# Loading, gating and splitting the first two token tiles ahead of their output products, and four staging halves for W_out

## The chip, the cores and the metric

The kernel runs on one core of a Trainium2 chip. The metric is the device time of one execution in microseconds (us). TensorE is called PE in the profile, VectorE DVE, ScalarE ACT, GpSimd POOL, SyncE SP; SP issues all the large transfers in this program and its queue is shown as SPq. The kernel before took 683.60, 685.08 and 685.92 us in three runs, median 685.08.

## The reference

One step of a one-layer hybrid encoder. Each token row of x is projected once into the queries, keys and values of three groups of heads and into a gate of 1024 columns; the three attentions give 256 + 512 + 256 mixed columns, and these times the gate go through W_out into a residual and a LayerNorm. Cut to what matters here:

```
mixed = concat([o_a (256), o_b (512), o_m (256)], -1)      # o_b: RMS-normed per head, times subln_g
y     = einsum('bse,ed->bsd', mixed * silu(gate), w_out)   # 1024 x 1024
out   = layer_norm(DEEPNORM_ALPHA * x + y, ln_g, ln_b)
```

There are 1024 prompt tokens and 128 sample tokens, so nine tiles of 128 tokens, t = 0 to 8 (tile 8 holds the sample). Everything is float32.

## The kernel before

Every product of float32 matrices is done as three PE products of halves: an operand is split into a "hi" part (a cast, done by ACT) and a "lo" part (operand minus hi, done by DVE or POOL), and hi*hi, lo*hi and hi*lo are added in PSUM. Attention runs over eight units of two heads in the order M0, B0 to B3, A0, A1, M1. While PE works on one unit, the projections of what comes next are merged into it as a filler (`merge`). The instructions are emitted in that order and a list scheduler then fixes the order on each engine; on the chip each engine takes its instructions strictly in that order and waits on semaphores.

The last unit, M1 (`attention_m`, slot 7 of the mixed columns), works in four pairs of token tiles. Per pair: scores on PE, a maximum on DVE (L747), exp on ACT (L749), transposes on PE (L457), a split of these (`pth`, `ptl`, L460 and L461), products with the values into the one PSUM room `po` (L659), and `close_pair`, in which ACT copies half of `po` (L641) and DVE adds the halves (L644), which makes `po` free for the next pair. M1's filler is: two gate blocks in three chunks of 384 tokens (L142 to L144), each ended by tanh and a multiplication and a store to DRAM (`gates<-t`, L432); after each chunk c a call `load_wout(c)`; then the output products of tiles 0 and 1 (`out_steps`). Tiles 2 to 8 follow in a plain loop.

An output tile needs, in this order: the gates (`gscr`) and the mixed columns of seven slots (`oscr`) loaded from DRAM (L982, L984), the RMS factors (L986); the four slots of group B scaled by these (L987, DVE); mixed times gate for slots 0 to 6 (L995, DVE for t < 2, POOL after); slot 7 from M1's output, which is still in SBUF (L998); then `whi` (cast, ACT, L992) and `wlo` (subtraction, DVE, L993). The PE products are L1028, 2 x 8 x 3 per tile, each 128x512; then the residual sum and the statistics (L1035, L1036) and `norm`.

```
 gt = sp.tile(..., tag="kc") if t == 0 else pp.tile(..., tag="p")     # L981
 mx = op_.tile(..., tag="tab0") if t == 0 else pp.tile(..., tag="p")  # L983
```

For t = 1 both live in the pool `p`, whose six rooms hold the attention's probabilities. `mixed(t)` with its loads is called by the first of a tile's eight filler steps (`start(t)`).

`load_wout(c)` (L1074 to L1083) loads three rows of 128 of W_out (two for c = 2) in halves of 128x512 into a staging room `wraw` with two buffers, casts each half on ACT (L1082) and subtracts on DVE (first half) or POOL (second half, L1083). The splits end in x's room, tag `x{h,l}{c}`, free once the gates of chunk c have used x.

Of the kernel before, what the change touches and what calls it, by code (L numbers as in the profile page):

```python
# [7 lines left out]
F32 = mybir.dt.float32  # L8
F32R = mybir.dt.float32r
AF = mybir.ActivationFunctionType  # L10
ALU = mybir.AluOpType
# [4 lines left out]
P = 128  # L16
KT = 8
NTOK = 1152
NPR = 1024
CH = 384  # L20
# [24 lines left out]
SP = mybir.EngineType.SP  # L45
GATES = [2, 3, 4, 5, 0, 1, 6, 7]
SWAP = [i ^ 1 for i in range(32)]


class Pool:  # L50
# [4 lines left out]
    def __init__(self, pool):  # L55
        self.pool = pool
# [6 lines left out]
def hybrid_step(tc, d, o):  # L63
    nc = tc.nc
# [5 lines left out]
    def f(ap):  # L70
        return ap.bitcast(F32)

    const = pool("const")
    wst = pool("wst", 2)
# [7 lines left out]
    oscr = dram.tile([9, P, 7, P], F32, tag="mixed")  # L82
    gscr = dram.tile([9, P, 8, P], F32, tag="gates")
    mkscr = dram.tile([P, 256], F32, tag="mk")
    mvscr = dram.tile([P, 256], F32, tag="mv")
    rscr = dram.tile([9, 4, P], F32, tag="rstd")
# [19 lines left out]
    op_ = pool("opnd")  # L106
# [77 lines left out]
        nc.vector.tensor_tensor(out=u.va[:, :, :, 64:128], in0=v, in1=f(u.va[:, :, :, 0:64]), op=ALU.subtract)  # L184

    xp = pool("xp", 1, side="right")
    xh, xl = zip(*[[xp.tile([P, KT, CH], F32R, tag=f"x{i}{c}") for i in "hl"] for c in range(3)])


    cos = op_.tile([P, NTOK], F32, tag="tab0")  # L190
# [784 lines left out]
        return out  # L975


    def mixed(t):

        ts_ = slice(t * P, (t + 1) * P)  # L980
        gt = sp.tile([P, KT, P], F32, tag="kc") if t == 0 else pp.tile([P, KT, P], F32, tag="p")  # L981
        nc.sync.dma_start(gt, gscr[t])  # L982
        mx = op_.tile([P, 7, P], F32, tag="tab0") if t == 0 else pp.tile([P, 7, P], F32, tag="p")  # L983
        nc.sync.dma_start(mx, oscr[t])  # L984
        rs = tmp.tile([P, 4, P], F32, tag="rs", bufs=2)
        nc.sync.dma_start(rs, rscr[t].rearrange("(o k) c -> o k c", o=1).broadcast_to([P, 4, P]))  # L986
        nc.vector.scalar_tensor_tensor(  # L987
            out=mx[:, 2:6], in0=mx[:, 2:6], scalar=subg, in1=rs, op0=ALU.mult, op1=ALU.mult)
        mh, ml = [wst.tile([P, KT, P], F32R, tag=tag) for tag in ("whi", "wlo")]

        def parts(k):
            nc.scalar.copy(mh[:, k], gt[:, k])  # L992
            nc.vector.tensor_tensor(out=ml[:, k], in0=gt[:, k], in1=f(mh[:, k]), op=ALU.subtract)  # L993

        (nc.vector if t < 2 else nc.gpsimd).tensor_tensor(out=gt[:, 0:7], in0=mx, in1=gt[:, 0:7], op=ALU.mult)  # L995

        def last():
            nc.vector.tensor_tensor(out=gt[:, 7], in0=units[7].out[:, ts_], in1=gt[:, 7], op=ALU.mult)  # L998
            parts(slice(7, 8) if t < 2 else slice(0, 8))

        if t < 2:
            parts(slice(0, 7))
        else:
            last()
        return mh, ml, last

    outs = {}

    def start(t):
        u = outs[t] = Unit()  # L1010
        u.m = mixed(t)
        u.st = small.tile([P, 3, 6], F32, tag="st", bufs=2)

    def residual(t):
        u = outs[t]
# [54 lines left out]


    woh, wol = {}, {}

    def load_wout(c):  # L1074
        room = [xp.tile([P, 3, 1024], F32R, tag=f"x{i}{c}") for i in "hl"]
        for k in range(3 * c, min(3 * c + 3, KT)):
            hi, lo = woh[k], wol[k] = [r[:, k - 3 * c] for r in room]
            for n in range(2):
                s = slice(512 * n, 512 * n + 512)
                raw = wst.tile([P, 512], F32, tag="wraw")  # L1080
                nc.sync.dma_start(raw, d["wout"][k, :, s])
                nc.scalar.copy(hi[:, s], raw)  # L1082
                (nc.gpsimd if n else nc.vector).tensor_tensor(out=lo[:, s], in0=raw, in1=f(hi[:, s]), op=ALU.subtract)  # L1083

    def out_steps(t, u):

        st = {}

        def go(k):
            if k == 0:  # L1090
                start(t)
                if t == 0:
                    scales()
                st["y"] = [ps_p.tile([P, 512], F32, tag="pp") for _ in CUTS]
            if k == KT - 1:
                outs[t].m[2]()
            for cut, y in zip(CUTS, st["y"]):
                products(t, cut, y, k)
            if k == KT - 1:
                residual(t)  # L1100
                for n, (cut, y) in enumerate(zip(CUTS, st["y"])):
                    add(t, n, cut, y)
                norm(t)

        steps = [(1.4, lambda k=k: go(k)) for k in range(KT - 1)]
        return steps + [(1.4, lambda: go(KT - 1), lambda: t // 2 in u.closed)]
# [8 lines left out]
    stages = []  # L1115
    late = []
    first = [q_of(units[0])] + [gate_block(next(gates)) for _ in range(NG[0])]
    for parts in zip(*first):
        for part in parts:
            emit(part)  # L1120
    for i, u in enumerate(units):
        nxt = units[i + 1] if i + 1 < len(units) else None
        emit(with_stages(sum(k_of(u), []), EV))
        if u.kind != "M":
            while stages:
                stage()
            flush_tiny()
        if u.kind == "B":
            vb, ve = v_block(u, 14 + u.idx, o["bvT"][u.idx], 0)
        elif u.kind == "A":  # L1130
            tables_a(u)
            vb, ve = v_block(u, 4 + u.idx, o["avT"][u.idx], 512)
        else:
            vb, ve = [], []
        more = []
        gs = [gate_block(next(gates)) for _ in range(NG[i] if i else 0)]
        if nxt:
            more += sum(sum(gs, []), [])
        if nxt:
            more += sum(q_of(nxt), [])  # L1140
            fill = vb + more[:4] + ve + more[4:]
            if i == 6:
                stages = sample_of(u)
                fill = fill[:ES] + with_stages(fill[ES:], EV)
            if u.kind == "M":
                fill = with_stages(fill, 8)
        else:

            fill = []
            for c in range(3):  # L1150
                for g in gs:
                    fill += g[c]
                fill.append((0.0, lambda c=c: load_wout(c)))
            fill += out_steps(0, u) + out_steps(1, u)

        def need(kt, u=u, fill=fill):
            while u.vdone <= kt // 3:
                fill.pop(0)[1]()

        main = {"M": lambda: attention_m(u), "B": lambda: attention_b(u, need), "A": lambda: attention_a(u, need)}[u.kind]()  # L1160
        merge(main, fill, LEAD if u.kind != "M" else 1.0, RR if nxt else RL)
        if i != 6:
            ended = late[:]
            late.clear()
            now = sample_of(u)
            stages = stages + now[:LW] + ended + now[LW:]
        else:
            while stages:
                stage()
            flush_tiny()  # L1170
    for t in range(2, 9):
        start(t)
        residual(t)
        for n, cut in enumerate(CUTS if t < 8 else TAIL):
            if stages:
                stage()
            piece(t, n, cut)
        norm(t)
# [84 lines left out]
```

## Time and profile before

| what | value |
|---|---|
| three runs | 683.60, 685.08, 685.92 us (median 685.08) |
| profiled execution | 685.8 us, span 684.0 us |
| PE busy in the span | 662.8 us (97%) |
| DVE, ACT, POOL busy | 472.6, 356.3, 233.5 us (69%, 52%, 34%) |
| PE products L1028, all tiles | 37.5 + 37.0 + 37.1 us in 288 matmuls |
| idle of PE ahead of L1028 | 4.5 us (released by ACT, `whi` L992) and 1.4 us (released by DVE) |

How to read it: each engine's busy time is a share of one span, so a share of 97% says that PE is the engine to look at, and not where its 3% are. The slices of the page, then the table of stretches, then the single instructions say where. In a row of the timeline the brackets give how long the engine was idle ahead of that instruction and what released it.

### The profile page before, as it was taken

How to read it: one execution, taken by the hardware profiler on the slowest of the kernel's cores; microseconds unless marked ns; L12 is line 12 of the kernel's file. 1: busy time of each engine (PE TensorE's matmuls, PEld its weight loads, DVE VectorE, ACT ScalarE, POOL GpSimd, SP SyncE). 2: the span in 40 equal slices, each digit the busy share in tenths (PEclk: the TensorE clock that was granted, in tenths of full speed). 3: DMA queues.
4: the chain of work that ended last, by engine and by line, in shares of the span. 5: the costliest groups of instructions: out<-in, count | busy, mean ns of one | idle time of the engine just before them, and what ended most of it. 6: DMA issues, size and time to landing. Idle time of an engine off the chain costs nothing. (4 is left out here: it accounts for less than half of the span.)

```text
span 684.0 us, 12210 instructions
## 1 busy us (share of the span) xinstructions
PE 662.8 (97%) x4306; PEld 614.2 (90%) x4306; DVE 472.6 (69%) x1169; ACT 356.3 (52%) x922; POOL 233.5 (34%) x282
## 2 busy tenths in 40 slices
PE   8899999999999999999999999999999996999995
PEld 7789999999999999999999999999999985787884
DVE  4869966796579856897566435673666678677854
ACT  5748845566446645565456535764566684111000
POOL 7654212632344224532323433323133231324102
PEclk9999999999999999999999999999999998899999
DMA  8761432121312222142302132233222648684411
GB/s 276 247 218 45 150 130 74 39 87 54 97 58 78 82 86 74 41 165 83 87 29 78 59 90 63 78 104 103 84 82 89 206 135 305 219 285 156 154 61 62
DMA packets 55694, 78.91 MB, mean 115 GB/s; under 512 B 9369, under 2 KB 33233, under 8 KB 55633
## 3 DMA queue, kind: packets, MB, share of 16 engines
q1 hardware_dynamic: 55632, 78.13, 34.6%
q8 instruction: 34, 0.56, 0.3%
q14 instruction: 28, 0.22, 0.1%
HBM read 57.69 MB, written 20.42 MB: 114 GB/s over the span
## 5 line engine op out<-in xcount | busy, mean ns | idle before, releaser
L143 PE MATMUL pp<-xl,whi 128*128 128x384 f32 x672 | 229.1, 341 | 2.6 <-DVE xl L200 1.8
L142 PE MATMUL pp<-xh,whi 128*128 128x384 f32 x672 | 230.5, 343 | 0.3 <-DVE qa L159 0.2
L144 PE MATMUL pp<-xh,wlo 128*128 128x384 f32 x672 | 228.9, 341 | 0.0
L143 PEld LDWEIGHTS pp<-xl,whi 128*128 128x128 f32 x672 | 126.6, 188 | 5.8 <-DVE xl L200 2.4
L142 PEld LDWEIGHTS pp<-xh,whi 128*128 128x128 f32 x672 | 126.4, 188 | 3.4 <-issue 0.7
L144 PEld LDWEIGHTS pp<-xh,wlo 128*128 128x128 f32 x672 | 126.4, 188 | 1.7 <-issue 0.2
L127 POOL TENSOR_TENSOR wlo<-wraw,whi 128x512 fp32r<-128x512 f32 x54 | 72.4, 1361 | 66.1 <-ACT whi L126 50.9
L586 ACT ACTIVATE p<-ps,nm 128x512 f32<-128x512 f32 (+3 forms) x96 | 55.2, 580 | 47.8 <-DVE nm L583 36.2
L444 PE MATMUL ps<-ka,qa 128*128 128x512 f32 (+4 forms) x176 | 58.5, 338 | 0.5 <-DVE nm L693 0.5
L445 PE MATMUL ps<-kl,qa 128*128 128x512 f32 (+4 forms) x176 | 57.3, 328 | 0.0
L457 PE MATMUL pt<-ident,p 128*128 128x128 f32 x332 | 55.0, 274 | 0.7 <-DVE p L526 0.6
L581 DVE TENSOR_REDUCE nm<-ps 128x1 f32<-128x512 f32 (+3 forms) x96 | 51.0, 549 | 1.6
L461 DVE TENSOR_TENSOR ptl<-pt,pth 128x512 fp32r<-128x512 f32 x56 | 38.2, 684 | 12.2 <-ACT pth L460 11.7
L457 PEld LDWEIGHTS pt<-ident,p 128*128 128x128 f32 x332 | 39.6, 141 | 4.4 <-DVE p L526 0.8
L701 POOL TENSOR_SCALAR p<-p,rs 128x640 f32<-128x640 f32 (+4 forms) x32 | 21.5, 676 | 64.3 <-DVE rs L700 58.7
L460 ACT CAST pth<-pt 128x512 fp32r<-128x512 f32 x56 | 32.6, 588 | 20.9 <-PE pt L457 19.9
L1028 PE MATMUL pp<-xh,whi 128*128 128x512 f32 (+1 forms) x96 | 37.5, 392 | 4.5 <-ACT whi L992 4.5
L1028 PE MATMUL pp<-xh,wlo 128*128 128x512 f32 (+1 forms) x96 | 37.0, 387 | 1.4 <-DVE rs L1051 1.4
L1028 PE MATMUL pp<-xl,whi 128*128 128x512 f32 (+1 forms) x96 | 37.1, 386 | 0.0
L992 ACT CAST whi<-p 128x1024 fp32r<-128x1024 f32 (+2 forms) x9 | 8.6, 954 | 53.5 <-PE pp L1028 42.9
L465 DVE TENSOR_TENSOR ptl<-pt,pth 128x256 fp32r<-128x256 f32 (+1 forms) x72 | 25.2, 352 | 15.8 <-ACT pth L464 15.2
L620 PE MATMUL po<-pth,va 128*128 128x256 f32 (+1 forms) x160 | 35.4, 285 | 0.0
(225 smaller groups left out, 1352.9 us busy)
## 6 DMA issues: line engine op xcount, KB each, us to landing
wraw<-in_win SPq DMA_DIRECT2D x54, 256.0 KB, 3.2
xr<-in_xT SPq DMA_DIRECT2D x12, 384.0 KB, 4.0
gates<-t SPq DMA_DIRECT2D x24, 192.0 KB, 2.2
qa<-in_xn SPq DMA_DIRECT2D x9, 512.0 KB, 5.0
wraw<-in_wout SPq DMA_DIRECT2D x16, 256.0 KB, 2.6
p<-gates SPq DMA_DIRECT2D x8, 512.0 KB
out_y<-qa SPq DMA_DIRECT2D x16, 256.0 KB, 2.3
mixed<-od SPq DMA_DIRECT2D x28, 128.0 KB, 1.8
```

Of the source, the lines that this page charges most:

```text
L127: eng.tensor_tensor(out=lo[:, h], in0=raw, in1=f(hi[:, h]), op=ALU.subtract)
L142: nc.tensor.matmul(ps, lhsT=w[0][:, k], rhs=xh_[:, k], start=(k == 0), stop=False)
L143: nc.tensor.matmul(ps, lhsT=w[0][:, k], rhs=xl_[:, k], start=False, stop=False)
L144: nc.tensor.matmul(ps, lhsT=w[1][:, k], rhs=xh_[:, k], start=False, stop=(k == KT - 1))
L444: nc.tensor.matmul(ps, lhsT=u.qa[h][:, qs], rhs=u.ka[h][:, k0 : k0 + n], start=True, stop=False)
L445: nc.tensor.matmul(ps, lhsT=u.qa[h][:, qs], rhs=kl[h][:, k0 : k0 + n], start=False, stop=True)
L457: nc.tensor.transpose(pt[:, t, q * P : (q + 1) * P], p[q][:, cols[t][q] : cols[t][q] + P], ident)
L461: nc.vector.tensor_tensor(out=lo, in0=pt, in1=f(hi), op=ALU.subtract)
L581: nc.vector.tensor_reduce(out=nm[:, m, c : c + 1], in_=ps[c][:, : b - a], axis=AX.X, op=ALU.max, negate=True)
L586: nc.scalar.activation(e[:, a:b], ps[c][:, : b - a], AF.Exp, bias=nm[:, m, 0:1], accum_out=rs[:, m, c : c + 1])
L620: nc.tensor.matmul(out, lhsT=a, rhs=b, start=(g == 0 and x == 0), stop=(g == j and x == len(mm) - 1))
L1028: nc.tensor.matmul(y, lhsT=a[:, k], rhs=b[k][:, s], start=(k == 0 and x == 0), stop=(k == KT - 1 and x == 2))
```

## The change

- `mixed(t)` and `start(t)` are taken apart: `load(t)` (rooms and transfers), `gated(t)` (the scaling by the RMS factors and mixed times gate for slots 0 to 6), `parts(t, k)` (cast and subtraction) and `last_unit(t)` (slot 7).
- For t = 0 and 1 these are emitted in M1's filler behind the gate chunks: the loads after chunk 0, the gating after chunk 1, the splits of slots 0 to 6 after chunk 2. The eighth step of a tile's products does slot 7 alone. For t = 2 to 8 all stands at the top of the loop as before.
- Tile 1's gates and mixed columns live in the two `qa` rooms of the pool `op_` and not in the pool `p`.
- x's first chunk is in two rooms, of six and of two k-tiles (`Joined`). The second, `r{h,l}0`, becomes two staging halves for W_out besides the two of `wraw`. W_out's rows go 2, 3, 3 over the three calls (before 3, 3, 2). `load_wout(c)` issues the first four loads of its rows, `split_wout(c)` casts, subtracts and issues the others.

The number of instructions is the same on each engine but for one more on DVE.

```
...
+class Joined:
+    def __init__(self, a, b, n):
+        self.a, self.b, self.n = a, b, n
+    def __getitem__(self, key):
+        k = key[1]
+        if isinstance(k, int):
+            return self.a[:, k] if k < self.n else self.b[:, k - self.n]
+        return self.a[:, k] if k.start < self.n else self.b[:, k.start - self.n : k.stop - self.n]
...
     xp = pool("xp", 1, side="right")
-    xh, xl = zip(*[[xp.tile([P, KT, CH], F32R, tag=f"x{i}{c}") for i in "hl"] for c in range(3)])
+    def x_room(i, c):
+        if c:
+            return xp.tile([P, KT, CH], F32R, tag=f"x{i}{c}")
+        return Joined(xp.tile([P, 6, CH], F32R, tag=f"x{i}0"), xp.tile([P, 2, CH], F32R, tag=f"r{i}0"), 6)
+    xh, xl = zip(*[[x_room(i, c) for i in "hl"] for c in range(3)])
...
-    def mixed(t):
-        ts_ = slice(t * P, (t + 1) * P)
-        gt = sp.tile([P, KT, P], F32, tag="kc") if t == 0 else pp.tile([P, KT, P], F32, tag="p")
-        nc.sync.dma_start(gt, gscr[t])
-        mx = op_.tile([P, 7, P], F32, tag="tab0") if t == 0 else pp.tile([P, 7, P], F32, tag="p")
-        nc.sync.dma_start(mx, oscr[t])
-        rs = tmp.tile([P, 4, P], F32, tag="rs", bufs=2)
-        nc.sync.dma_start(rs, rscr[t].rearrange("(o k) c -> o k c", o=1).broadcast_to([P, 4, P]))
+    def load(t):
+        u = outs[t] = Unit()
+        if t == 0:
+            u.gt, u.mx = sp.tile([P, KT, P], F32, tag="kc"), op_.tile([P, 7, P], F32, tag="tab0")
+        elif t == 1:
+            u.gt, u.mx = [op_.tile([P, KT, P], F32, tag=f"qa{i}", bufs=2) for i in range(2)]
+            u.mx = u.mx[:, 0:7]
+        else:
+            u.gt, u.mx = pp.tile([P, KT, P], F32, tag="p"), pp.tile([P, 7, P], F32, tag="p")
+        nc.sync.dma_start(u.gt, gscr[t])
+        nc.sync.dma_start(u.mx, oscr[t])
+        u.rs = tmp.tile([P, 4, P], F32, tag="rs", bufs=2)
+        nc.sync.dma_start(u.rs, rscr[t].rearrange("(o k) c -> o k c", o=1).broadcast_to([P, 4, P]))
+        u.st = small.tile([P, 3, 6], F32, tag="st", bufs=2)
+    def gated(t):
+        u = outs[t]
         nc.vector.scalar_tensor_tensor(
-            out=mx[:, 2:6], in0=mx[:, 2:6], scalar=subg, in1=rs, op0=ALU.mult, op1=ALU.mult)
-        mh, ml = [wst.tile([P, KT, P], F32R, tag=tag) for tag in ("whi", "wlo")]
-        def parts(k):
-            nc.scalar.copy(mh[:, k], gt[:, k])
-            nc.vector.tensor_tensor(out=ml[:, k], in0=gt[:, k], in1=f(mh[:, k]), op=ALU.subtract)
-        (nc.vector if t < 2 else nc.gpsimd).tensor_tensor(out=gt[:, 0:7], in0=mx, in1=gt[:, 0:7], op=ALU.mult)
-        def last():
-            nc.vector.tensor_tensor(out=gt[:, 7], in0=units[7].out[:, ts_], in1=gt[:, 7], op=ALU.mult)
-            parts(slice(7, 8) if t < 2 else slice(0, 8))
-        if t < 2:
-            parts(slice(0, 7))
-        else:
-            last()
-        return mh, ml, last
+            out=u.mx[:, 2:6], in0=u.mx[:, 2:6], scalar=subg, in1=u.rs, op0=ALU.mult, op1=ALU.mult)
+        (nc.vector if t < 2 else nc.gpsimd).tensor_tensor(out=u.gt[:, 0:7], in0=u.mx, in1=u.gt[:, 0:7], op=ALU.mult)
+    def parts(t, k):
+        u = outs[t]
+        if k.start == 0:
+            u.m = [wst.tile([P, KT, P], F32R, tag=tag) for tag in ("whi", "wlo")]
+        mh, ml = u.m
+        nc.scalar.copy(mh[:, k], u.gt[:, k])
+        nc.vector.tensor_tensor(out=ml[:, k], in0=u.gt[:, k], in1=f(mh[:, k]), op=ALU.subtract)
+    def last_unit(t):
+        gt = outs[t].gt
+        nc.vector.tensor_tensor(out=gt[:, 7], in0=units[7].out[:, t * P : (t + 1) * P], in1=gt[:, 7], op=ALU.mult)
-    def start(t):
-        u = outs[t] = Unit()
-        u.m = mixed(t)
-        u.st = small.tile([P, 3, 6], F32, tag="st", bufs=2)
...
     woh, wol = {}, {}
+    ROWS = [(0, 2), (2, 5), (5, 8)]
+    raws = {}
+    def load_half(i):
+        if i % 2:
+            raws[i] = xp.tile([P, 512], F32, tag=f"r{'hl'[i // 2 % 2]}0")
+        else:
+            raws[i] = wst.tile([P, 512], F32, tag="wraw")
+        n = i % 2
+        nc.sync.dma_start(raws[i], d["wout"][i // 2, :, 512 * n : 512 * n + 512])
     def load_wout(c):
-        room = [xp.tile([P, 3, 1024], F32R, tag=f"x{i}{c}") for i in "hl"]
-        for k in range(3 * c, min(3 * c + 3, KT)):
-            hi, lo = woh[k], wol[k] = [r[:, k - 3 * c] for r in room]
-            for n in range(2):
-                s = slice(512 * n, 512 * n + 512)
-                raw = wst.tile([P, 512], F32, tag="wraw")
-                nc.sync.dma_start(raw, d["wout"][k, :, s])
-                nc.scalar.copy(hi[:, s], raw)
-                (nc.gpsimd if n else nc.vector).tensor_tensor(out=lo[:, s], in0=raw, in1=f(hi[:, s]), op=ALU.subtract)
+        a, b = ROWS[c]
+        room = [xp.tile([P, b - a, 1024], F32R, tag=f"x{i}{c}") for i in "hl"]
+        for k in range(a, b):
+            woh[k], wol[k] = [r[:, k - a] for r in room]
+        for i in range(2 * a, 2 * a + 4):
+            load_half(i)
+    def split_wout(c):
+        a, b = ROWS[c]
+        for i in range(2 * a, 2 * b):
+            k, n = i // 2, i % 2
+            s = slice(512 * n, 512 * n + 512)
+            nc.scalar.copy(woh[k][:, s], raws[i])
+            (nc.gpsimd if n else nc.vector).tensor_tensor(
+                out=wol[k][:, s], in0=raws[i], in1=f(woh[k][:, s]), op=ALU.subtract)
+            if i + 4 < 2 * b:
+                load_half(i + 4)
...
             if k == 0:
-                start(t)
                 if t == 0:
             if k == KT - 1:
-                outs[t].m[2]()
+                last_unit(t)
+                parts(t, slice(7, 8))
             for cut, y in zip(CUTS, st["y"]):
...
             fill = []
+            todo = [
+                lambda: (load_wout(0), load(0), load(1), split_wout(0)),
+                lambda: (load_wout(1), gated(0), gated(1), split_wout(1)),
+                lambda: (parts(0, slice(0, 7)), load_wout(2), parts(1, slice(0, 7)), split_wout(2)),
+            ]
             for c in range(3):
                     fill += g[c]
-                fill.append((0.0, lambda c=c: load_wout(c)))
+                fill.append((0.0, todo[c]))
             fill += out_steps(0, u) + out_steps(1, u)
...
     for t in range(2, 9):
-        start(t)
+        load(t)
+        gated(t)
+        last_unit(t)
+        parts(t, slice(0, 8))
         residual(t)
```

PE at the end of M1. Here `pp` are the output tiles' PSUM rooms, `po` a pair's, `pt` transposes; tile 1's operands are whi_9495 and wlo_9496 before and whi_9349 and wlo_9350 in the changed kernel. Before:

```order
L457 MATMUL pt_9515<-ident_81,p_9408 128x128
L1028 MATMUL pp_9501<-xh_1403_8930,whi_9495 128x512
L1028 MATMUL pp_9501<-xl_1404_8931,whi_9495 128x512
L1028 MATMUL pp_9502<-xh_1403_8930,whi_9495 128x512
L1028 MATMUL pp_9502<-xl_1404_8931,whi_9495 128x512
L659 MATMUL po_9524<-pth_9453,va_8754 128x256
```

And in the changed kernel:

```order
L476 MATMUL pt_9517<-ident_81,p_9423 128x128
L1049 MATMUL pp_9503<-xh_1405_8932,whi_9349 128x512
L1049 MATMUL pp_9503<-xl_1406_8933,whi_9349 128x512
L1049 MATMUL pp_9503<-xh_1405_8932,wlo_9350 128x512
L1049 MATMUL pp_9503<-xh_1405_8932,whi_9349 128x512
L1049 MATMUL pp_9503<-xl_1406_8933,whi_9349 128x512
L1049 MATMUL pp_9503<-xh_1405_8932,wlo_9350 128x512
```

Tile 1's products stand at the same place; before, the four that need only `whi` come first and M1's last products follow, and now each k-tile's three stand together.

DVE during the gates' last chunks. `kc` and `tab` hold tile 0's gates and mixed columns, the two `qa` tile 1's, `nm` is a maximum over scores. Before:

```order
L995 TENSOR_TENSOR kc_9341<-tab_1471_9343,kc_9341 128x896
L465 TENSOR_TENSOR ptl_8513<-pt_8511,pth_8512 128x128
L747 TENSOR_REDUCE nm_9001<-ps_9003 128x1
L431 SCALAR_TENSOR_TENSOR t_1422_9038<-t_1422_9038,pp_8956 128x384
L521 RECIPROCAL rs_8868<-rs_8868 128x1
```

And in the changed kernel:

```order
L450 SCALAR_TENSOR_TENSOR t_1430_9046<-t_1430_9046,pp_8964 128x384
L484 TENSOR_TENSOR ptl_8515<-pt_8513,pth_8514 128x128
L1018 TENSOR_TENSOR kc_8942<-tab_1412_8943,kc_8942 128x896
L766 TENSOR_REDUCE nm_9009<-ps_9011 128x1
L540 RECIPROCAL rs_8870<-rs_8870 128x1
L540 RECIPROCAL rs_8878<-rs_8878 128x1
L1018 TENSOR_TENSOR qa_1415_8949<-qa_1416_8950,qa_1415_8949 128x896
L545 TENSOR_SCALAR p_8865<-p_8865,rs_8870 128x256
```

Tile 1's gating has come forward to tile 0's, and both now stand around the same reduction.

DVE where M1's second pair is closed (the add into `tab_1379`; L644 before, L663 after). Before, p_9488 and p_9490 are tile 1's rooms and p_9594 is tile 2's:

```order
L644 TENSOR_TENSOR tab_1377_8757<-po_9197,po_1456_9272 64x256 x2
L461 TENSOR_TENSOR ptl_9374<-pt_9372,pth_9373 128x512
L461 TENSOR_TENSOR ptl_9389<-pt_9387,pth_9388 128x512
L998 TENSOR_TENSOR p_9488<-tab_1377_8757,p_9488 128x128
L993 TENSOR_TENSOR wlo_9496<-p_9488,whi_9495 128x128
L1035 SCALAR_TENSOR_TENSOR qa_1498_9472<-qa_1497_9470,pp_9358 128x512
L987 SCALAR_TENSOR_TENSOR p_9490<-p_9490,subg_92,rs_9492 128x512
```

In the changed kernel, where p_9597 is tile 2's room for the mixed columns:

```order
L1031 TENSOR_TENSOR qa_1415_8949<-tab_1379_8759,qa_1415_8949 128x128
L1026 TENSOR_TENSOR wlo_9336<-kc_8942,whi_9335 128x128
L1026 TENSOR_TENSOR wlo_9350<-qa_1415_8949,whi_9349 128x128
L480 TENSOR_TENSOR ptl_9389<-pt_9387,pth_9388 128x512
L1016 SCALAR_TENSOR_TENSOR p_9597<-p_9597,subg_92,rs_9600 128x512
L663 TENSOR_TENSOR tab_1379_8759<-po_9209,po_1464_9284 64x256 x2
L480 TENSOR_TENSOR ptl_9404<-pt_9402,pth_9403 128x512
```

Tile 1's scaling is gone from here, and tile 2's scaling now stands ahead of the second pair's close.

## Rows read from the trace of the kernel before

**Rows 1.** The page's 40 slices: busy tenths of PE, granted clock in tenths.

```profile
PE   8899999999999999999999999999999996999995
PEclk9999999999999999999999999999999998899999
```

**Rows 2.** Stretches (us): length, busy (x) of PE PEld DVE ACT POOL, clock, DMA, GB/s.

```profile
532.00:540.00 8.00, 8.00 (x56) 7.93 (x55) 6.59 (x18) 5.84 (x17) 1.29 (x1) 1.00 0.74 240
566.00:570.00 4.00, 3.78 (x17) 2.71 (x15) 2.03 (x6) 2.99 (x9) 1.30 (x1) 1.00 0.88 323
570.00:572.70 2.70, 2.25 (x16) 1.86 (x16) 1.81 (x5) 0.78 (x3) 0.00 (x0) 1.00 1.03 419
572.70:577.20 4.50, 0.02 (x1) 0.00 (x0) 4.50 (x9) 2.35 (x4) 0.00 (x0) 0.80 0.56 151
577.20:581.00 3.80, 3.73 (x12) 3.10 (x12) 3.75 (x7) 0.01 (x1) 1.69 (x1) 0.50 1.01 396
581.00:582.40 1.40, 0.04 (x1) 0.00 (x0) 1.40 (x3) 1.27 (x2) 0.40 (x1) 0.50 0.99 398
582.40:585.80 3.40, 3.40 (x8) 2.70 (x9) 3.35 (x8) 0.26 (x1) 1.01 (x1) 0.53 0.84 291
585.80:594.30 8.50, 8.50 (x38) 6.78 (x36) 2.58 (x5) 0.00 (x0) 2.12 (x1) 1.00 0.69 233
```

**Rows 3.** PE timeline around tile 1's first products: start, busy us, idle before and releaser.

```profile
577.26 0.79 PE L1028 MATMUL pp<-xh,whi 128*128 128x512 f32 x1 [4.54 <-ACT whi L992]
578.28 0.63 PE L1028 MATMUL pp<-xh,whi 128*128 128x512 f32 x1
578.71 0.63 PE L1028 MATMUL pp<-xl,whi 128*128 128x512 f32 x1
582.40 1.22 PE L1028 MATMUL pp<-xh,wlo 128*128 128x512 f32 x2 [1.36 <-DVE rs L1051]
```

**Rows 4.** Timeline of SP: tile 1's and tile 0's loads, and one later.

```profile
531.47 0.32 SPq L982 DMA_DIRECT2D kc<-gates  x1
...
564.20 0.42 SPq L982 DMA_DIRECT2D p<-gates  x1
...
622.88 0.42 SPq L984 DMA_DIRECT2D p<-mixed  x1
```

**Rows 5.** Timeline of DVE: gating, closing and splitting.

```profile
535.45 1.09 DVE L995 TENSOR_TENSOR kc<-tab,kc 128x896 f32<-128x896 f32 x1 [1.11 <-DMA kc<-gates]
550.73 1.08 DVE L993 TENSOR_TENSOR wlo<-kc,whi 128x896 fp32r<-128x896 f32 x1
569.18 0.85 DVE L644 TENSOR_TENSOR tab<-po,po 64x256 f32<-64x256 f32 x2 [1.25 <-ACT po L641]
571.84 0.29 DVE L998 TENSOR_TENSOR p<-tab,p 128x128 f32<-128x128 f32 x1 [0.49 <-DMA p<-gates]
573.30 0.74 DVE L987 SCALAR_TENSOR_TENSOR p<-p,subg,rs 128x512 f32<-128x512 f32 x1
579.81 2.54 DVE L993 TENSOR_TENSOR wlo<-p,whi 128x896 fp32r<-128x896 f32 x1
627.27 0.75 DVE L987 SCALAR_TENSOR_TENSOR p<-p,subg,rs 128x512 f32<-128x512 f32 x1 [3.59 <-DMA p<-mixed]
```

**Rows 6.** Timeline of ACT: tile 1's cast.

```profile
576.27 0.94 ACT L992 CAST whi<-p 128x896 fp32r<-128x896 f32 x1 [2.11 <-DVE p L995]
```

**Rows 7.** Timeline of POOL: the gating of tile 2.

```profile
579.31 2.09 POOL L995 TENSOR_TENSOR p<-p,p 128x896 f32<-128x896 f32 x1 [11.79 <-DVE p L987]
```

**Rows 8.** Chain that ended last: start us, length us, what.

```profile
582.42 12.00 PE pp L1028 x44
...
625.40 5.63 PE pp L1028 x24
```

**Rows 9.** DMA issues: what, queue, count, KB each, median us to landing.

```profile
p<-mixed SPq DMA_DIRECT2D x8, 448.0 KB, 7.6
```

**Rows 10.** POOL by line and form, 500 to 684 us: W_out's splits.

```profile
L1083 POOL TENSOR_TENSOR xl<-wraw,xh 128x512 fp32r<-128x512 f32 x8 | 10.3, 1293 | 35.6 <-ACT xh L1082 35.6
```

More of the change, by code (lines that the diff above doesn't have):

```diff
@@ L1117, in hybrid_step @@
     first = [q_of(units[0])] + [gate_block(next(gates)) for _ in range(NG[0])]
-    for parts in zip(*first):
-        for part in parts:
+    for row in zip(*first):
+        for part in row:
             emit(part)
```

## The prediction

> **What bounds the kernel now.** I read the page's slices first, then the table of stretches, then PE's single instructions, then what released them. In the slices PE is at 8 or 9 tenths everywhere but in one, the 34th, which shows 6, and in the last; the clock shows 8 in the 34th and the 35th [rows 1]. A slice is 17.1 us long, so the place lies between 564 and 598 us, where M1 ends and tile 1's products begin. The stretches split it [rows 2]. PE is idle for 0.22 + 0.45 + 4.48 + 0.07 + 1.36 = 6.58 us from 566 to 582.4 us. From 577.2 to 585.8 us the granted clock is 0.50 to 0.53, the lower of the two levels (1.2 against 2.4 GHz); it fell after the idle 4.5 us and was back at 1.00 from 585.8 us on. PE is busy there for 3.73 + 0.04 + 3.40 = 7.17 us. What the low level costs is read from the spacing of the same 128x512 matmul: 578.71 - 578.28 = 0.43 us there [rows 3], and 5.63 / 24 = 0.235 us in the chain [rows 8]. So 45% of the 7.17 us, or 3.2 us, is lost to the clock. At stake is 6.6 + 3.2 = 9.8 us, and no more: from 582.42 us on the chain is made of PE's products [rows 8], with nothing that this change could shorten.
>
> Why PE stands: its wait of 4.54 us is released by ACT's cast `whi` [rows 3], which waited 2.11 us for DVE's L995 [rows 6], which follows L987 at 573.30 us, and that was queued behind L998 at 571.84 us, which waited for tile 1's gates [rows 5]. Their transfer was issued at 564.20 us [rows 4], so it took 7.6 us to land, at DMA shares of 0.88 to 1.03 [rows 2]. It could not be issued earlier since both loads of tile 1 are in the pool `p`, whose rooms hold M1's probabilities till then. The second wait, 1.36 us, is for `wlo`: the profile names `rs` L1051, but the subtraction that PE needs runs just ahead of it, 2.54 us from 579.81 us [rows 5].
>
> **The change part by part.** *Tile 1 early.* The loads go to the `qa` rooms, free since A1, and the gating and the splits stand under the gate chunks. At the end of M1 nothing of this is left but slot 7, 0.28 us for each of two DVE instructions and a short cast, ahead of a pair that PE still has to work on. Both waits and the low clock go: -9.8 us. The moved instructions themselves (0.75, 1.09, 1.08 us on DVE, 0.94 on ACT [rows 5, 6]) cost nothing by their length, since PE had no gap around tile 0's own ones (8.00 of 8.00 us busy from 532 to 540 us, while DVE was busy for 6.6 and ACT for 5.8 us [rows 2]).
>
> *What is late next, place one: gating both tiles.* SP holds the two loads of gates together, behind a W_out half that waits for a staging room. On DVE the two L1018 instructions stand around a maximum and ahead of the normalisation of a pair's probabilities; whoever waits for gates there stops M1's exp and its transposes. In the trace before, tile 0's gates were issued at 531.47 us and were there at 535.45 us, after 4.0 us [rows 4, 5]; DVE stood idle for 1.11 us for them, and PE lost nothing. New are the second load (512 KB, 1.2 us at the 419 GB/s of the busiest stretch [rows 2]) and the second instruction of 1.09 us, 2.3 us together. The lower bound is 0, what the row of tile 0 cost. The upper is what a landing after 7.6 us would add to one after 4.0 us: 3.6 us. The nearest row is tile 0's, so I take little: 0.3 us.
>
> *Place two: the close of M1's second pair.* Here the order of DVE gets worse. Tile 2's scaling (L1016) now stands ahead of the add that frees `po` (L663, before L644). DVE's queue behind L1016 is that add and a `ptl`, and PE's products of the third pair need both. Tile 2's loads need rooms of the pool `p` that come free with a set of four transposes on PE. From there PE has 15 output products (15 x 0.235 = 3.5 us [rows 8]), twelve transposes and one pair's products, which I put at 2.0 us, so 5.5 us in hand. The chain against it: the gates' issue 0.42 us [rows 4], the mixed columns' landing, 0.75 us for L1016 and 0.85 us for the close [rows 5]. Landing has two rows: 627.27 - 622.88 = 4.4 us, where DVE waited 3.59 us for just this transfer [rows 4, 5], and the median of 7.6 us for this kind [rows 9]. With 4.4 us the chain is 6.4 us, with some 0.3 us for the hand-overs 6.7, and PE waits for 1.2 to 1.3 us. With 7.6 us it waits for 4.4 us. The lower bound is 0 (a landing within 3 us). I take 1.3 us: at 622.88 us the loads of one tile were issued together, as they are here, and the 7.6 us belong to a queue with two tiles' loads in it. At 1.3 us I count no loss of clock, since waits of 0.2 to 0.5 us left it at 1.00 and the 4.5 us did not [rows 2]; the bound is that it falls as it did, 3.2 us.
>
> *Tile 0's residual.* x's rows for tile 0 are now loaded just ahead of tile 2's, and its additions (L1056) stand behind the close. They free the two PSUM rooms that tile 1's products start in. By the same steps the first addition ends 2.0 us after the close is there, where PE has some 1.9 us of M1 in hand: 0.3 us with the hand-overs, 0 at best, and with the late landing it is part of the 4.4 us.
>
> *W_out's staging and x's two rooms.* ACT casts W_out's halves in other groups, the same number of casts, subtractions and loads. With four halves the loads wait less. M1's exps stand behind two casts in a row at one place (2 x 0.6 us); with ACT busy for 5.8 of 8 us and PE without a gap around there [rows 2] I count 0. It would be 1.2 us for each place if PE had no slack.
>
> The Trainium skill, page "SBUF — State Buffer", section "Who interferes with whom", states that a DVE instruction with two inputs in SBUF and a GpSimd instruction that reads SBUF shut each other out for their whole length. The trace agrees: the subtraction of 896 columns took 1.08 us alone and 2.54 us where POOL's gating of 2.09 us ran beside it [rows 5, 7]. This speaks against the change, which puts two gatings and two subtractions of DVE among POOL's eight W_out splits of 1.29 us [rows 10]. By it place one could cost up to 1.3 us more, and the sum below would be 6.6 us.
>
> **The sum.** -9.8 + 0.3 + 1.3 + 0.3 = -7.9 us. Against the profiled execution: 685.8 - 7.9 = 677.9 us. That execution stands 0.7 us above the median of the three runs, so against the median the forecast is 685.08 - 7.9 = 677.2 us.
>
> **The rivals.** *A: tile 2's loads land late.* For it: the 7.6 us of most such transfers [rows 9], and three transfers of 448 to 512 KB issued together. Against it: the 4.4 us. Then PE waits for 4.4 us at place two, its clock falls as it did before, 3.2 us, and of 9.8 us there remain 9.8 - 0.3 - 4.4 - 3.2 = 1.9 us: 683.2 us.
>
> *B, slower: both places are caught by late landings.* The gates of tiles 0 and 1 also land 7.6 us after issue, so place one costs 3.6 us with 3.2 us for the clock, and place two 4.4 with 3.2: 14.4 against 9.8 us, 4.6 us slower, 689.7 us. It decides from the point at which the added waits of PE, the clock's part included, exceed 9.8 us. For it: DMA shares of 0.74 around 532 to 540 us [rows 2], with W_out's halves now bunched in fours. Against it: tile 0's gates landed in 4.0 us in that very stretch.
>
> *C: the change doesn't do what it says.* Tile 1's splits are emitted early but come late, since ACT's cast stands behind W_out's halves that wait for staging rooms; then the wait for `whi` is there as before, for 685 us. Against it: the cast stands ahead of all of tile 0's products on PE's side, more than 10 us before it is needed.
>
> *D: place two costs nothing*, because the loads are there in time: 9.8 - 0.3 = 9.5 us, 675.6 us.
>
> **How the numbers follow.** The forecast, with all between 675.9 and 680 us (one of the small costs is doubled or the clock falls once): 0.55. D: 0.10. A, with all between 680 and 684.5 us: 0.20. C: 0.06. B: 0.09. What a measurement of this kernel can tell from no change is about 0.3%, 2.05 us, so faster means below 683.0 us and slower above 687.1 us. Faster holds the forecast, D and two thirds of A: 0.78. Same holds the rest of A, C, and a share of B in which only one place is full: 0.13. Slower is the rest of B: 0.09. The range goes from 674.8 us (D, less the spread of the runs) to 683.4 us (A); the forecast's own range is 675.9 to 680 us.
>
> **What would show it.** In the profile of the changed kernel tile 1's products, L1049, follow M1's last products without an idle time above 0.5 us and at clock 1.00, and the slice with 6 tenths is gone. L1016 of tile 2 shows an idle time on DVE released by `p<-mixed`, and PE's third pair, L678, one of about 1.3 us behind it, released by L663. The loads of both tiles' gates land about 4 us after issue, and PE stays whole between 530 and 550 us. From tile 2's first product to the end all takes as long as before. The prediction is wrong if a new gap of over 2 us stands at either place, if the clock falls in M1, or if the wait for `whi` is still there.

## The result, and the profile after

The changed kernel took 676.29 us (median of four runs, 675.73 to 679.49) against 685.50 us for the kernel before (four runs, 683.60 to 685.99): 0.9873 of its time, 95% interval 0.9843 to 0.9903. Run again later it gave 0.9863 (0.9840 to 0.9886). The forecast was 677.2 us. The profiled execution took 675.73 us, with a span of 673.9 us; from the profiled execution of the kernel before, the forecast was 677.9 us.

The page's slices, PE and its granted clock, as in [rows 1]:

```profile
PE   9899999999999999999999999999999999999995
PEclk9999999999999999999999999999999999999998
```

The slice with 6 tenths is gone, and so are the two slices of lower clock at M1's end. The stretches of M1's end, columns as in [rows 2]:

```profile
565.00:570.00 5.00, 4.90 (x31) 3.94 (x29) 4.31 (x12) 3.54 (x8) 0.27 (x1) 1.00 0.74 242
570.00:575.00 5.00, 4.50 (x25) 3.95 (x26) 4.96 (x10) 2.71 (x4) 1.84 (x1) 1.00 0.98 303
575.00:580.00 5.00, 5.00 (x24) 4.06 (x23) 3.64 (x9) 0.00 (x0) 1.01 (x1) 1.00 0.99 367
```

PE is idle for 0.10 and 0.50 us where it was idle for 6.6 us, and the clock stays at 1.00. The PE timeline has one wait from 520 to 600 us, at the third pair of M1, and tile 1's products follow M1's instructions without one:

```profile
569.30 0.60 PE L476 MATMUL pt<-ident,p 128*128 128x128 f32 x4
570.50 0.35 PE L678 MATMUL po<-pth,va 128*128 128x256 f32 x1 [0.60 <-DVE tab L663]
...
571.90 0.48 PE L1049 MATMUL pp<-xh,whi 128*128 128x512 f32 x1
572.21 0.40 PE L1049 MATMUL pp<-xl,whi 128*128 128x512 f32 x1
```

Tile 1 and tile 0 on DVE (gating L1018, subtraction L1026), which answer to [rows 5]:

```profile
538.02 1.09 DVE L1018 TENSOR_TENSOR kc<-tab,kc 128x896 f32<-128x896 f32 x1 [2.07 <-DMA kc<-gates]
539.79 1.09 DVE L1018 TENSOR_TENSOR qa<-qa,qa 128x896 f32<-128x896 f32 x1 [0.21 <-DMA qa<-gates]
549.57 1.08 DVE L1026 TENSOR_TENSOR wlo<-kc,whi 128x896 fp32r<-128x896 f32 x1
554.60 1.09 DVE L1026 TENSOR_TENSOR wlo<-qa,whi 128x896 fp32r<-128x896 f32 x1
...
568.25 0.69 DVE L480 TENSOR_TENSOR ptl<-pt,pth 128x512 fp32r<-128x512 f32 x1 [0.20 <-ACT pth L479]
568.86 0.74 DVE L1016 SCALAR_TENSOR_TENSOR p<-p,subg,rs 128x512 f32<-128x512 f32 x1
569.52 0.84 DVE L663 TENSOR_TENSOR tab<-po,po 64x256 f32<-64x256 f32 x2
```

And the loads behind them, on SP:

```profile
533.92 0.33 SPq L1007 DMA_DIRECT2D kc<-gates  x1
534.30 0.42 SPq L1007 DMA_DIRECT2D qa<-gates  x1
...
564.27 0.38 SPq L1008 DMA_DIRECT2D p<-mixed  x1
```

In what follows a landing is the time from a transfer's issue to the start of the instruction that needs it; where that instruction did not wait for it, the landing is at most that long. The gates landed 4.1 us (tile 0) and 5.5 us (tile 1) after issue. DVE waited 2.07 and 0.21 us for them, and PE had no wait: from 530 to 540 us it was busy for 10.00 us. Tile 1's subtraction was done at 555.7 us, 16 us ahead of the product that reads it. L1016 found tile 2's mixed columns there 4.6 us after issue, without a wait.

The whole gain lies in one stage. From one and the same transpose in M1 (`pt<-ident,se`, at 525.45 us before and 525.38 us after) to the start of tile 2's products it is 68.81 us before (to 594.26 us) and 58.78 us after (to 584.16 us): 10.03 us less. From there to PE's last product both take 81.88 us. I summed PE's rows of that stage, each from its start to the next one's, less the idle time in brackets:

| | before | after |
|---|---|---|
| idle | 6.57 us | 0.60 us |
| output products, `pp` (201) | 44.54 us, 222 ns each | 41.77 us, 208 ns each |
| M1's products, `po` (64) | 8.94 us, 140 ns each | 7.63 us, 119 ns each |
| scores and transposes | 8.76 us | 8.78 us |

So 5.97 us came from waits and 4.06 us from the pace. Between two runs of the changed kernel this stage with the rest differs by 0.9 us (140.66 and 141.56 us to the last product), so single tenths mean nothing.

### The profile page after: what moved, and what is told of

Same layout as the page of the kernel before. It is cut to its first block, busy times and chain, and to the rows that moved or that the text cites. A ratio compares the mean times of both kernels' runs of the same rounds, so it can differ in the third digit from the quotient of the medians.

```text
span 673.9 us, 12216 instructions
## 1 busy us (share of the span) xinstructions
PE 660.9 (98%) x4306; PEld 614.8 (91%) x4306; DVE 473.7 (70%) x1169; ACT 356.3 (53%) x922; POOL 235.1 (35%) x282
## 4 chain that ended last, share of the span: by engine, by line
PE 85%; DVE 7%; DMA 4%; issue 1%; ACT 1%; SPq 1%; POOL 0%; POOLq 0%; DVEq 0%; ACTq 0%
PE pp L155 16%; PE pp L156 16%; PE pp L157 16%; PE pp L1049 8%; PE ps L1049 6%; PE pt L476 4%; PE po L639 4%; PE ps L463 4%; PE ps L464 4%; PE po L678 3%; PE pt L891 1%; PE ps L806 1%; DVE xl L219 1%; DVE p L545 1%; PE pt L427 1%
## 5 line engine op out<-in xcount | busy, mean ns | idle before, releaser
L155 PE MATMUL pp<-xh,whi 128*128 128x384 f32 x616 | 211.5, 343 | 0.2 <-DVE qa L172 0.2
L156 PE MATMUL pp<-xl,whi 128*128 128x384 f32 x616 | 209.8, 341 | 1.8 <-DVE xl L219 1.8
L157 PE MATMUL pp<-xh,wlo 128*128 128x384 f32 x616 | 209.8, 341 | 0.0
L156 PEld LDWEIGHTS pp<-xl,whi 128*128 128x128 f32 x616 | 115.9, 188 | 4.6 <-DVE xl L219 2.4
L155 PEld LDWEIGHTS pp<-xh,whi 128*128 128x128 f32 x616 | 115.9, 188 | 3.2 <-issue 0.7
L157 PEld LDWEIGHTS pp<-xh,wlo 128*128 128x128 f32 x616 | 115.9, 188 | 1.6 <-issue 0.2
L463 PEld LDWEIGHTS ps<-ka,qa 128*128 128x128 f32 x176 | 33.2, 189 | 2.0 <-DVE nm L712 0.7
```

Source lines behind the costliest of these rows:

```text
L155: nc.tensor.matmul(ps, lhsT=w[0][:, k], rhs=xh_[:, k], start=(k == 0), stop=False)
L156: nc.tensor.matmul(ps, lhsT=w[0][:, k], rhs=xl_[:, k], start=False, stop=False)
L157: nc.tensor.matmul(ps, lhsT=w[1][:, k], rhs=xh_[:, k], start=False, stop=(k == KT - 1))
L463: nc.tensor.matmul(ps, lhsT=u.qa[h][:, qs], rhs=u.ka[h][:, k0 : k0 + n], start=True, stop=False)
```

## The experiments

The forecast put all of the gain on tile 1's early loads and nothing on W_out's staging. The first four runs take the change apart. "The stage" below is the time from that same transpose in M1 to PE's last product: 150.69 us before, 140.66 us after.

**Rooms only.** The kernel before, with

```
+ gt = ... op_.tile([P, KT, P], F32, tag="qa0", bufs=2) if t == 1 ...
+ mx = ... op_.tile([P, KT, P], F32, tag="qa1", bufs=2)[:, 0:7] if t == 1 ...
```

> The kernel before with one edit: tile 1's gates and mixed columns live in the two qa rooms, and the call stays where it was, in the first of the tile's eight filler steps. Theory (the time of tile 1's transfers decides, and that follows from the place of the call as much as from the room): the loads are still issued after 560 us, the mixed columns even behind tile 2's loads, so the wait for whi stays, 4 to 7 us with the clock at its lower level after it: 684 to 689 us. Rival (the room in the pool p was what held the loads): they are issued before 545 us, PE has no wait over 1 us at tile 1's products, 676 to 678 us.

687.57 us, 1.0022 of before (1.0006 to 1.0037). On PE:

```profile
577.46 0.55 PE L659 MATMUL po<-pth,va 128*128 128x256 f32 x1 [4.39 <-DVE tab L644]
582.17 0.80 PE L1028 MATMUL pp<-xh,whi 128*128 128x512 f32 x1 [2.67 <-ACT whi L992]
```

The gates were issued at 564.12 us and the mixed columns at 566.92 us, behind tile 2's. The room alone gives nothing where the call stays: the theory's side by the time and by the issue. The waits have another form than was expected: 2.67 us are for `whi`, and the longer one is for the close of M1's second pair, which stood on DVE behind tile 0's residual and tile 2's scaling:

```profile
573.42 0.75 DVE L987 SCALAR_TENSOR_TENSOR p<-p,subg,rs 128x512 f32<-128x512 f32 x1 [0.23 <-DMA p<-mixed]
...
576.47 0.84 DVE L644 TENSOR_TENSOR tab<-po,po 64x256 f32<-64x256 f32 x2
```

**Staging only.** The kernel before, with `Joined`, `x_room`, `ROWS`, `load_half` and `split_wout` of the change, and

```
- fill.append((0.0, lambda c=c: load_wout(c)))
+ fill.append((0.0, lambda c=c: (load_wout(c), split_wout(c))))
```

> The kernel before with the other half of the change: x's first chunk in two rooms, four staging halves for W_out, its rows 2, 3, 3; tile 1 is loaded and gated as before. Theory: tile 1's loads are still issued after 560 us and its splits late, PE waits 4 to 6 us in all at M1's end and the clock falls: 683 to 689 us. Rival (the staging gives a good part of the 9 us, since W_out's loads held up SP's queue): under 682 us.

678.12 us, 0.9873 (0.9844 to 0.9902): the theory failed here, and clearly. By time this half alone can't be told from the whole change; by the profile its stage is 144.09 us, 6.6 of the 10.0 us. The profiled execution, at 680.80 us, was the slowest of the four (the others took 677.59 to 678.30 us). SP, DVE and PE:

```profile
560.93 0.46 SPq L1150 DMA_DIRECT2D ka<-in_ln_b  x1
561.49 0.40 SPq L1035 DMA_DIRECT2D qa<-in_xn  x1
565.65 0.33 SPq L1000 DMA_DIRECT2D p<-gates  x1
...
572.04 0.38 SPq L1000 DMA_DIRECT2D p<-gates  x1
...
569.28 0.29 DVE L1016 TENSOR_TENSOR p<-tab,p 128x128 f32<-128x128 f32 x1 [1.24 <-DMA p<-gates]
570.85 0.75 DVE L1005 SCALAR_TENSOR_TENSOR p<-p,subg,rs 128x512 f32<-128x512 f32 x1 [0.62 <-DMA p<-mixed]
...
572.26 0.66 PE L475 MATMUL pt<-ident,p 128*128 128x128 f32 x4 [0.73 <-DVE ptl L479]
574.11 0.46 PE L677 MATMUL po<-pth,va 128*128 128x256 f32 x1 [1.19 <-DVE tab L662]
```

In the kernel before, SP's queue around tile 1's gates (issued at 564.20 us [rows 4]):

```profile
563.29 0.38 SPq L1113 DMA_DIRECT2D ka<-in_ln_b  x1
563.73 0.42 SPq L1017 DMA_DIRECT2D qa<-in_xn  x1
...
565.26 0.57 SPq L982 DMA_DIRECT2D p<-gates  x1
```

Tile 1's gates are issued as late as before, but land in 3.6 us where it was 7.6 us [rows 4, 5]. Before, ln_b and x's rows were issued just ahead of them; here they are 4 to 5 us ahead. So it is how long the transfer takes that decides as much as when it is issued. But more than one thing has moved: tile 2's gates, issued 1.1 us behind tile 1's before, come 6.4 us behind them here, and PE has M1's third pair (574.11 us) ahead of tile 1's first products (575.22 us), where before the products stood first.

**Early, but in the pool `p`.** The changed kernel without its `elif t == 1` branch.

> The changed kernel with tile 1's gates and mixed columns in the pool p as before the change, but loaded at the early place. M1's probabilities have four rooms of six from then on. Theory: early transfers are enough, 676 to 679 us, and the idle of PE from 530 us to tile 2's first product stays under 2 us. Rival (the qa rooms are needed, since M1's pairs can no longer overlap): PE waits 0.5 us or more at each of three pairs or its clock falls, 679 to 685 us.

679.11 us, 0.9902 (0.9867 to 0.9937), on the rival's side by a little. Two waits of PE:

```profile
553.26 0.50 PE L1046 MATMUL pp<-xh,whi 128*128 128x512 f32 x1 [1.75 <-DVE t L450]
571.34 0.35 PE L678 MATMUL po<-pth,va 128*128 128x256 f32 x1 [1.79 <-DVE tab L663]
```

The first is a queue on DVE: a gate's multiplication stood behind tile 1's scaling, which waited 2.09 us for its mixed columns (issued at 544.51 us, when a room came free). The clock fell to 0.72 from 570 to 575 us. By the medians the `qa` rooms are worth 2 to 3 us, in that the loads are 5 to 27 us earlier; the intervals of the two kernels overlap.

**Early only.** The changed kernel with the old `load_wout` and x in one room per chunk.

> The changed kernel with W_out loaded and split as before the change (two staging halves, rows 3, 3, 2, x in one room per chunk); loads, gating and splits of tiles 0 and 1 stay early and in the qa rooms. Theory: all of the gain comes from tile 1's early transfers, 675 to 678 us, PE idle from 530 us to tile 2's first product 0.5 to 1.5 us. Rival (the staging halves matter: with two, tile 1's gates queue behind W_out's halves and whi of tile 0 or W_out's rows come late): idle of 3 us or more, 679 to 685 us.

681.67 us, 0.9930 (0.9904 to 0.9956): the rival's side. ACT and PE:

```profile
572.15 0.62 ACT L1084 CAST xh<-wraw 128x512 fp32r<-128x512 f32 x1 [1.33 <-DMA wraw<-in_wout]
...
572.82 0.79 PE L1031 MATMUL pp<-xh,whi 128*128 128x512 f32 x1 [1.58 <-ACT xh L1084]
574.03 1.11 PE L458 MATMUL pt<-ident,p 128*128 128x128 f32 x4 [0.42 <-DVE ptl L462]
```

W_out's last half was issued at 566.86 us, after ln_b, x's rows and tile 2's gates, and landed 5.3 us later; the clock fell to 0.50 from 572.8 us on and was 0.57 from 575 to 580 us. With two staging halves the wait for tile 1 turns into one for W_out.

**Place two.** The changed kernel, run again, and one with

```
+ if t == 2:
+     nc.gpsimd.tensor_scalar_mul(u.mx[:, 2:6], u.mx[:, 2:6], subg)
+     nc.gpsimd.tensor_tensor(out=u.mx[:, 2:6], in0=u.mx[:, 2:6], in1=u.rs, op=ALU.mult)
```

> The changed kernel itself, run beside the next one for a direct comparison. Both theories: 675.5 to 677 us, PE idle 0.6 us from 525 us to tile 2's first product.

> The changed kernel with tile 2's scaling (L1016) done by POOL in two instructions, so that on DVE nothing of tile 2 stands ahead of the close of M1's second pair. Theory (the 0.6 us for which PE still waits at the third pair is the 0.7 us that L1016 itself takes on DVE, not a landing): the wait goes or falls below 0.1 us, 0.4 to 0.7 us less than the changed kernel, 675.6 us. Rival (the close is late by itself, from the transposes' split and ACT's copy ahead of it): the wait stays at 0.4 us or more and the time is the same within 0.2 us.

676.63 and 676.62 us, 0.9863 each (0.9840 to 0.9886 and to 0.9887). The stretch from 570 to 575 us, of the first and of the second:

```profile
570.00:575.00 5.00, 4.39 (x28) 3.66 (x27) 4.96 (x11) 3.14 (x5) 2.11 (x1) 1.00 0.78 270
```

```profile
570.00:575.00 5.00, 5.00 (x34) 4.33 (x33) 4.60 (x11) 3.74 (x8) 3.59 (x3) 1.00 0.73 256
```

The 0.61 us at the third pair go when L1016 leaves DVE, so it was the instruction's own length. The time did not move, against the theory: 0.6 us is a tenth of a per cent, less than these intervals tell, and a wait of 0.45 us stood at 542.49 us in that run. The changed kernel's own second run had a wait of 0.26 us at 549.25 us beside the 0.61 us, 0.87 us in all where 0.6 was expected. This is no version that is shown to be better.

**What makes the landing long.** Three runs with the kernel before. The first leaves out two transfers ahead of tile 1's gates:

```
+ if w == "ln_b": norms.append(norms[0]); continue
+ if t: u.xn = outs[0].xn; return
```

> The kernel before without two transfers of 512 KB that SP issues just ahead of tile 1's gates: ln_b isn't loaded (ln_g is used in its place) and x's rows are loaded for tile 0 alone and used for all tiles. W_out's staging and tile 1's rooms and place are as before. Theory after the first four runs (tile 1's gates land late since SP, held by W_out's staging, then issues six transfers at once, and a transfer waits for the bytes ahead of it): they land 4.5 to 5.5 us after issue in place of 7.6 us, PE's wait for whi falls to 1 to 3 us, 677 to 682 us. Rival (the landing is slow for another reason, the place or the rooms): 7 us or more, 684 to 687 us.

683.50 us, 0.9970 (0.9955 to 0.9985). SP's issue and the DVE instruction that needs the gates:

```profile
563.12 0.38 SPq L982 DMA_DIRECT2D p<-gates  x1
...
568.27 0.28 DVE L998 TENSOR_TENSOR p<-tab,p 128x128 f32<-128x128 f32 x1
569.60 0.85 DVE L644 TENSOR_TENSOR tab<-po,po 64x256 f32<-64x256 f32 x2 [1.05 <-ACT po L641]
...
571.88 0.75 DVE L987 SCALAR_TENSOR_TENSOR p<-p,subg,rs 128x512 f32<-128x512 f32 x1
```

The landing is at most 5.2 us, without a wait of DVE, as the theory expected. The gain of 2 us is less than the least that was expected: PE still waits 1.72 us for `whi` and 1.72 us for `wlo`. The gates are there by 568.27 us, but DVE scales tile 1's mixed columns only at 571.88 us, behind the close of M1's second pair and two splits. A shorter landing alone is therefore worth little here. DVE's order isn't quite that of the kernel before either: tile 0's residual, which stood ahead of tile 1's gating, stands behind it here.

The second moves 512 KB behind tile 1's loads elsewhere (`tag="qa0"` for tile 2's gates).

> The kernel before with tile 2's gates in a qa room, so that their 512 KB are issued later and not right behind tile 1's loads; the order on DVE at M1's end is the same as before. If transfers are served in the order of issue, what is behind does not count: tile 1's gates land after 7 to 7.6 us as before, 684 to 686 us. If all transfers in flight share the engines, 1.2 us less: 6.0 to 6.5 us, 682 to 684 us.

683.91 us, 0.9974 (0.9959 to 0.9988).

```profile
565.88 0.42 SPq L982 DMA_DIRECT2D p<-gates  x1
...
573.38 0.29 DVE L998 TENSOR_TENSOR p<-tab,p 128x128 f32<-128x128 f32 x1 [0.42 <-DMA p<-gates]
...
578.81 0.80 PE L1028 MATMUL pp<-xh,whi 128*128 128x512 f32 x1 [4.48 <-ACT whi L992]
```

7.5 us, as before, and the wait for `whi` is the same. But a load of 512 KB of the sample's keys moved up to 567.70 us, so the bytes behind fell less than meant: inconclusive on what is behind. What the run gained is the wait of 1.36 us for `wlo`, which is gone.

The third leaves out W_out's last row, which I thought held SP's queue:

```
+ if k == 7: woh[7], wol[7] = woh[6], wol[6]; continue
```

> The kernel before without the loads and splits of W_out's last 128 rows (the seventh row's are used twice); on DVE the order from the close of M1's second pair on is the same as before. Theory (with two staging halves the last loads of W_out hold SP's queue until 563 us, so that ln_b, x's rows and tile 1's loads are issued in one burst): SP issues ln_b and x's rows 2 us or more ahead of tile 1's gates, these land within 6 us of issue in place of 7.6 us, PE's wait for whi falls below 3 us, 678 to 682 us. Rival (the burst comes from the rooms of the pool p that come free at 564 us, and W_out has no part in it): landing 7 us or more, wait 4 us or more, 683 to 686 us.

684.18 us, 0.9972 (0.9960 to 0.9985). What SP's queue waited for (us, times, longest), then the timeline:

```profile
SPq L1116 <- PE ps L445: 3.2, 1, 3.2
```

```profile
562.66 0.33 SPq L1116 DMA_DIRECT2D ka<-in_ln_b  x1
563.03 0.43 SPq L1017 DMA_DIRECT2D qa<-in_xn  x1
563.51 0.43 SPq L982 DMA_DIRECT2D p<-gates  x1
...
576.64 0.51 PE L1028 MATMUL pp<-xh,whi 128*128 128x512 f32 x1 [3.93 <-ACT whi L992]
```

This theory fell. The landing was at most 7.7 us (DVE came to the gates at 571.23 us, without a wait), and the wait for `whi` lay between the two expectations. SP was free, and ln_b then waited 3.2 us for M1's last scores on PE, whose keys stand in its room; the burst formed all the same. With the new staging the scheduler also sets those scores otherwise: in the run with staging only, one head's stand at 559.28 us and the other's at 564.54 us, and before all four at 561.54 to 561.89 us. That order, and not a free queue, goes with ln_b's issue 4.7 us ahead of the gates. No run here isolates it.

**Early, with W_out short.** The same edit in the kernel with early loads and the old staging.

> The early loads with W_out's old staging, without the loads and splits of W_out's last 128 rows. Theory (what that kernel lost against the whole change is the late landing of W_out's last halves, which tile 0's last k-tile needs): the 1.6 us wait for W_out's cast and the lower clock behind it go, 675.5 to 678 us. Rival (the early loads hold SP and DVE at other places too): 679 us or more.

679.99 us (678.11 to 682.44), 0.9912 (0.9888 to 0.9937), outside what the theory expected by the median, and on the rival's side. By the profile, whose execution was the fastest of the four (678.11 us), the wait for W_out's cast is gone and the clock stays at 1.00. What is left is the wait that the prediction priced at place two, in just its form:

```profile
563.39 0.42 SPq L990 DMA_DIRECT2D p<-mixed  x1
...
570.19 0.75 DVE L998 SCALAR_TENSOR_TENSOR p<-p,subg,rs 128x512 f32<-128x512 f32 x1 [1.24 <-DMA p<-mixed]
...
571.60 0.66 PE L458 MATMUL pt<-ident,p 128*128 128x128 f32 x4 [1.23 <-DVE ptl L462]
572.45 0.35 PE L660 MATMUL po<-pth,va 128*128 128x256 f32 x1 [0.19 <-DVE tab L645]
```

Tile 2's scaling waits for its load, 6.8 us from issue, and the split and the close behind it are late by as much: 1.42 us of PE. PE also waited 0.77 us at 559.10 us.

## Why the prediction was right

- **The sum.** By the profiles the gain is 10.0 us where 7.9 was forecast, by the medians 9.2 us. Two terms make the difference of 2.1 us: the pace gave 0.8 us more than forecast, and of the 1.9 us that were put down for places one and two and the residual only 0.6 us came. The median, 676.29 us, lies between the forecast and rival D (675.6 us, no cost at place two), and it can't be told which of the two is nearer.
- **What is at stake, 9.8 us.** Right in place and nearly in size. All of the 6.57 us idle are gone (the 0.60 us that are left are place two's). The pace gave 4.06 us, where the forecast had 3.2 us for the clock. PE's work from 577.26 to 585.83 us took 7.2 us without the wait in it, and at the spacing of the changed kernel's last stretch of M1 (236 ns for an output product, 123 ns for one of M1's) it would take 3.8 us: 3.4 us is the clock. The other 0.7 us are spread over rows at full clock, and what they come from was not measured.
- **Why the loads were late.** The forecast put it down to the pool `p`, whose rooms come free late. That was not enough: with the rooms changed alone the gates were still issued at 564.12 us. The change also moves the call, so the forecast did not suffer from it.
- **Place one, 0.3 us.** 0. Landings of 4.1 and 5.5 us lie in the lower half of the forecast's 4.0 to 7.6 us; DVE stood idle for 2.28 us, and PE for none.
- **Place two, 1.3 us.** 0.60 us, and not by the landing: the load was there in time, and PE waited for the length of L1016 itself, since the wait goes when POOL does that work. The queue on DVE was the right mechanism. The chain from the four transposes (their end at 563.68 us) to the third pair (570.50 us) took 6.8 us, as forecast (6.7 us), but PE had 6.2 us of work in hand and not 5.5: that term was mis-sized by 0.7 us. In the last run, with a landing of 6.8 us, the wait for the load did cost PE 1.42 us.
- **Tile 0's residual, 0.3 us.** 0: the additions ended at 572.3 us and tile 1's products had started at 571.90 us, in the PSUM room that the first of the two had freed.
- **The rule on DVE and GpSimd.** The forecast took it from the Trainium skill, page "SBUF — State Buffer", section "Who interferes with whom": a DVE instruction with two inputs in SBUF contends with a GpSimd instruction that reads SBUF. The four moved instructions took 1.08 to 1.09 us, as long as alone, and the 1.3 us that were priced by the rule did not arise. That the rule is wrong doesn't follow, for these four met no split: POOL's stood from 532.55 to 533.85, 544.55 to 547.55, 550.83 to 552.12 and 556.51 to 558.36 us. Where DVE and POOL did meet in the same trace, a W_out split on DVE took 1.37 us (from 545.02 us), and one that met none 0.69 us.
- **W_out's staging, 0.** This step failed, though the sum did not show it. The forecast counted what the staging costs (casts in a row) and not what it does to the order: with it alone tile 1's gates landed in 3.6 us, PE's idle time in the stage fell from 6.57 to 2.58 us, and the time was 0.9873 of before. So most of the gain can be had with tile 1's loads issued as late as ever. Which part of the new order does it is not shown: taking away 1 MB ahead of the gates brought the landing to at most 5.2 us but only 2 us of time. The early start without the new staging gave 0.993, 681.67 us, since W_out's last halves then came late, and that is outside the forecast's own range of 675.9 to 680 us. All the credit thus went to the half that gives less by itself, and that the sum came out is partly luck: the change does both, and the two cover one and the same loss.
- **The rivals.** A (683 us) and B did not come. C did not either: tile 1's splits ended at 555.7 us. With the early loads and the old staging ACT's casts did wait for W_out's halves, as C had it, but what came late was W_out's own cast (572.15 us) and not tile 1's.

## What to carry to other kernels

A transfer that lands late can be issued earlier or have less around it in the queue; price both before crediting one part of a change with the gain, and look whether the engine that needs it comes to it at once (here a landing 2.4 us shorter gave 2 us of some 9). Where two parts of a change answer to one wait, their gains don't add: test each alone. And look at what stands behind an instruction in its engine's queue as well as at its own wait, since it is the close behind it that PE waits for.

## What the runs showed that was not expected

- PE's clock fell to its lower level after 4.5 us of idle time before, but also after 0.73 and 1.19 us close together (0.74 from 575 to 580 us, staging only) and after 1.58 us (0.50 from 572.8 to 574 us, early only). It stayed at 1.00 after 0.60 us, after 1.23 and 0.19 us in the last run, and after a single wait of 1.75 us (at 553.26 us, early but in the pool `p`); in that same run it fell after 1.79 us at 571.34 us. So in these runs the length of a wait alone does not tell what happens to the clock, and the forecast's choice of no loss at 1.3 us was not safe.
- The same kind of transfer of 448 to 512 KB landed 3.6, 4.1, 5.5, 6.8 and 7.6 us after issue in these runs. That what is issued ahead of it matters was tested once (7.6 against at most 5.2 us); what is issued behind it was not settled.
